# A gated convolution's input projection: c and u of tiles 2 to 5 by seven block products in place of plain products

## The chip, the cores and the metric

The kernel runs on one core of one Trainium2 chip. A time is the device time of one execution in microseconds (us). Of the kernel before there are three timed runs, 1012.52, 1012.60 and 1012.88 us, with a median of 1012.6. One more execution was recorded by the hardware profiler. Engines are called as the profile calls them: PE (TensorE), PEld (its weight loads), DVE (VectorE), ACT (ScalarE), POOL (GpSimd), SP (SyncE, which only issues loads here).

## The reference

The model has two layers of width 1024 on 512 tokens, in float32. The change lies in the first mixer, of which only the projection by `w_in` is computed in another way:

```python
def short_conv_mixer(h, w_in, conv_w, w_out):      # h = rmsnorm(x, a_pre_norm)
    bcx = h @ w_in                                 # 512x1024 @ 1024x3072
    b_gate, c_gate, u = jnp.split(bcx, 3, axis=-1)
    y = b_gate * causal_depthwise_conv3(c_gate * u, conv_w)
    return y @ w_out
# layer 0: h = h + rmsnorm(short_conv_mixer(...)); h = h + rmsnorm(swiglu(rmsnorm(h)))
# layer 1: k, v from rmsnorm(h) @ w_kv; sliding-window attention with sinks; swiglu
```

## The kernel before, in words

**Arithmetic.** A product of float32 matrices is made of three matmuls in the 32-bit round format: each operand is split into a rounded high part and the remainder, and `mm3` issues weight-high by x-low, weight-high by x-high, weight-low by x-high. The high part of a weight block (128x1024, 512 KB) is a copy on ACT (`whi<-raw`, L490 before), the low part a subtraction on DVE (`wlo<-raw,whi`, L491). A plain job is `project`: eight depth blocks by three, 24 matmuls of 128 weight columns against 512 tokens, into one PSUM bank of 128x512.

**The convolution's tiles.** The 1024 columns of c, u and b are cut in eight tiles f of 128 columns, which lie on partitions with the 512 tokens beside them. For each tile there are a c, a u and a b job. Behind them stand the steps of `conv`: `first` multiplies c's bank by the row factor `rows` (1 over the root mean square of each token's x, broadcast over the partitions by two matmuls into the bank `pr`), `second` does the same for u and forms cu = c times u, `taps` makes the three taps of the causal convolution on DVE (a scaling and two multiply-adds), `third` multiplies b's bank by `rows` and forms y. The two products cu and y run on GpSimd for the tiles 0 to 6 (`eng`). Tiles 0 and 1 are projected in the opening, while the first loads arrive, and their steps are left for the list `late`.

**The line.** The jobs of the tiles 2 to 7 stand in one line, in the order of the string `CONV`, with the products P1 to P7 of the first half of `w_out` (these were block products before already, made by `seven` with sums of y from `pair_sums`) and the splits w0 to w3 of the second half of `w_out` between. `in_line` walks it: after the products of job j it splits the weights of job j + 3 (`LINE_LEAD`), issues the loads whose buffer the job just split used last (seven raw buffers of 512 KB, `raw`), sums raw blocks for the job behind that one (`add`), takes a few steps from `late`, and then appends job j's own steps to `late`. There are four pairs of split weights. PSUM's banks come from three pools: `ps_mm` four, `ps_sc` two, `ps_pt` two.

**Order.** All engines run under a schedule written by hand: what the program writes first for an engine runs first on it. Weight loads are issued on SP's queue. GpSimd's queue also issues `hsum` transfers: copies and accumulations from DRAM to DRAM that make sums of blocks of the feed-forward weights `w_gb` and `w_dn` for later (class `Sums`, `sum_on`, `issue`, L559 before). In the convolution's line `sum_on(f"c{f}")` puts a group in the list, and `issue` writes it at once.

Of the kernel before, what the change touches and what calls it, by code (L numbers as in the profile page):

```python
# [16 lines left out]
P = 128  # L17
D = 1024
# [19 lines left out]
    "c2 u2 b2 c3 u3 b3 c4 u4 b4 c5 u5 P1 P5 b5 P6 P3 c6 P7 P2 u6 P4 b6 w0 c7 u7 w1 b7 w2 w3"  # L38
)

# [41 lines left out]
def yoco_kernel(  # L82
# [8 lines left out]
    w_in: bass.AP,  # L91
    w_ob: bass.AP,
# [134 lines left out]
    xt = [halves("xt") for _ in range(KT // 2)]  # L227
    xt = [xt[k // 2][k % 2] for k in range(KT)]
# [217 lines left out]
    class Raw:  # L446


        def __init__(self, *srcs):
            self.srcs = srcs  # L450
            self.widths = [s.shape[0] * S if len(s.shape) == 3 else D for s in srcs]
            self.n = sum(self.widths)

        def fetch(self):
            self.tile, c = wraw.tile([P, D], F32, tag="raw", name=name("raw")), 0
            for src, n in zip(self.srcs, self.widths):
                dst = self.tile[:, c : c + n]
                if len(src.shape) == 3:
                    src, dst = (src.rearrange("k p c -> p k c"),
                                dst.rearrange("p (k c) -> p k c", c=S))  # L460
                nc.sync.dma_start(dst, src)
                c += n

    class Job:
# [10 lines left out]
        def add(self):  # L475
            if self.make:
# [18 lines left out]
    def in_line(jobs, late, paced=True):  # L495
# [9 lines left out]
        def prepare(j):  # L505
# [3 lines left out]
            while n[0] < len(raws) and (n[0] < N_RAW or raws[n[0] - N_RAW].last <= j):  # L509
                raws[n[0]].fetch()  # L510
# [7 lines left out]
        for j, job in enumerate(jobs):  # L518
# [5 lines left out]
            for _ in range(1 if paced else max(len(late) - 1, 1)):  # L524
# [143 lines left out]
    rows = slot("rrow")  # L668
# [6 lines left out]
    sums = small.tile([P, 4], F32, tag="sums", name=name("sums"))  # L675
    squares = wide("squares")

    def square(b):
        nc.scalar.activation(squares, hs[b], AF.Square, scale=1 / 32,
                             accum_out=sums[:, b : b + 1])  # L680

    with tc.manual_schedule(engines=ALL):

        warm = small.tile([P, 1], F32, tag="warm", name=name("warm"))
        nc.scalar.activation(warm, ones[:, 0:1], AF.Copy)
        idle = bank("idle", ps_pt)
        for _ in range(WARM):
            nc.tensor.matmul(idle[:, :P], ones, ones, start=True, stop=True)

        def first_hi(i, c0, c1):  # L690
            nc.scalar.activation(ws[i][0][:, c0:c1], first[i][:, c0:c1], AF.Copy)

        def first_lo(i, c0, c1):
            nc.vector.tensor_tensor(out=ws[i][1][:, c0:c1], in0=first[i][:, c0:c1],
                                    in1=ws[i][0][:, c0:c1].bitcast(F32), op=ALU.subtract)

        def token_hi(k):
            nc.scalar.activation(xs[k][0], xt[k], AF.Copy, scale=g(G_APRE, k))

        def token_lo(k):  # L700
            nc.vector.scalar_tensor_tensor(
                out=xs[k][1], in0=xt[k], scalar=g(G_APRE, k), in1=xs[k][0].bitcast(F32),
                op0=ALU.mult, op1=ALU.subtract,
            )

        FIRST = {0: [(0, 0, P), (0, P, 384)], 1: [(0, 384, 768)], 2: [(0, 768, D), (1, 0, S)],
                 4: [(1, S, D)], 5: [(2, 0, S)], 6: [(2, S, D)]}
        for k in range(KT):
            pieces = FIRST.get(k, [])
            token_hi(k)  # L710
            for p in pieces:
                first_hi(*p)
            for p in pieces:
                first_lo(*p)
            token_lo(k)
            for i in range(3):
                for t in range(3):
                    n = 3 * k + t
                    whi, wlo = (w[:, n % KT * P : (n % KT + 1) * P] for w in ws[n // KT])
                    nc.tensor.matmul(begun[0][t], (whi, wlo, whi)[i], xs[k][i == 2],  # L720
                                     start=k == i == 0, stop=k == KT - 1 and i == 2)
        later += [fetch(w_in[1, t]) for t in range(len(later), 3)]
        for b in range(NB):
            hs[b] = wide("h")
            nc.sync.dma_start(hs[b], x[b])
        nc.sync.dma_start(mask, tables[:, 2 * S :])
        nc.sync.dma_start(snk, sinks.partition_broadcast(P))
        ws = [split_weights(None, raw, True) for raw in later[:2]]
        square(0)
        square(1)  # L730
        ws.append(split_weights(None, later[2], True))
        square(2)
        square(3)
        project(begun[1][0], ws[0], xs)
        v = small.tile([P, 4], F32, tag="v", name=name("v"))
        nc.vector.tensor_scalar(out=v, in0=sums, scalar1=EPS, scalar2=None, op0=ALU.add)
        nc.gpsimd.tensor_tensor(out=cols, in0=v, in1=mhalf, op=ALU.pow)
        project(begun[1][1], ws[1], xs)
        pr = bank("pr", ps_pt)
        dg, dhi, dlo = slot("dg"), slot("dhi", F32R), slot("dlo", F32R)  # L740
        for b in range(NB):
            nc.vector.tensor_scalar(out=dg[:, b * P : (b + 1) * P], in0=ident,
                                    scalar1=cols[:, b : b + 1], scalar2=None, op0=ALU.mult)
        nc.scalar.activation(dhi, dg, AF.Copy)
        nc.vector.tensor_tensor(out=dlo, in0=dg, in1=dhi.bitcast(F32), op=ALU.subtract)
        nc.tensor.matmul(pr, ones_r, dlo, start=True, stop=False)
        nc.tensor.matmul(pr, ones_r, dhi, start=False, stop=True)
        nc.scalar.activation(rows, pr, AF.Copy)
        nc.vector.tensor_scalar(out=nsnk, in0=snk, scalar1=-1.0, scalar2=None, op0=ALU.mult)
# [5 lines left out]
    def conv(f, pc=None, pu=None, pb=None):  # L755

        eng = nc.gpsimd if f < KT - 1 else nc.vector
        cr, ur = halves("cru")
        cu, t = halves("cut")
        br, y = halves("bry")  # L760
# [8 lines left out]
        def second(pu):  # L769
            nc.vector.tensor_tensor(out=ur, in0=pu, in1=rows, op=ALU.mult)  # L770
            eng.tensor_tensor(out=cu, in0=cr, in1=ur, op=ALU.mult)

        def taps():
            nc.vector.tensor_scalar(out=t, in0=cu, scalar1=g(G_CONV, 16 + f), scalar2=None,
                                    op0=ALU.mult)
# [6 lines left out]
        def third(pb):  # L782
            nc.vector.tensor_tensor(out=br, in0=pb, in1=rows, op=ALU.mult)
            eng.tensor_tensor(out=y, in0=t, in1=br, op=ALU.mult)
# [14 lines left out]

        return first, second, taps, third, end  # L800

# [34 lines left out]
    with tc.manual_schedule(engines=ALL):  # L836
        project(begun[1][2], ws[2], xs)

        def late():
            parts = []  # L840
            for f in range(2):
                first, second, taps, third, end = conv(f)
                first(begun[f][0])
                second(begun[f][1])
                parts += [taps, lambda third=third, f=f: third(begun[f][2])]
                sum_on(f"c{f}")
                issue(len(issues))
# [899 lines left out]
```

## Time and profile before

| what | value |
|---|---|
| runs, median (lowest to highest) | 1012.6 us (1012.52 to 1012.88) |
| the profiled execution | 1012.5 us; its span on the chip 1010.7 us |
| granted clock of TensorE, mean | 0.999 |
| instructions | 16083 |
| moved by DMA | 244.50 MB, 242 GB/s |
| GpSimd's transfers (software queue) | 96.48 MB, 37.6% of 16 engines' span |
| hardware queue of the loads | 145.98 MB, 38.8% |

The profile is of one execution. The span goes from the first to the last instruction recorded; what is not in it (1.8 us) lies around it. Busy times are sums of instruction times, and matmuls are pipelined, so one matmul's time is longer than the distance to the next; the distance between two starts, called pitch here, is what a matmul costs. A row of an engine in order of time gives the start, the length, the engine, the line, the operation, out<-in by the program's names, and the shape; in square brackets stands how long the engine was idle ahead of it and what ended that. A row of DMA issues gives the median time from issue to landing.

### The profile page before, as it was taken

To read this page: it belongs to the slowest core of one execution; us is meant where nothing else is said; L and a number is where in the kernel's file an instruction comes from. 1 tells how busy PE (TensorE), PEld (TensorE's weight loads), DVE (VectorE), ACT (ScalarE), POOL (GpSimd) and SP (SyncE) were. 2 spreads that over 40 slices of the span, in tenths; PEclk is the share of its full clock that TensorE was granted. 3 is DMA by queue.
4 is the path that set the end of the run, shared out by engine and by line. 5 is a ranking of instruction groups with operands and counts; after the bars stand their busy time and mean duration, and the time that the engine had idled before them with its cause. 6 is when DMAs were issued, how large, how long until landed. Compare 5 with 4: busy or idle time off the path is not lost.

```text
span 1010.7 us, 16083 instructions
## 1 busy us (share of the span) xinstructions
PE 1002.3 (99%) x5864; PEld 882.4 (87%) x5864; DVE 887.7 (88%) x1525; ACT 588.4 (58%) x1061; POOL 203.9 (20%) x264
## 2 busy tenths in 40 slices
PE   9999999999999999999999999999999999999997
PEld 8888888999889898898898888789998888989986
DVE  5766767899789999999888998888997999999996
ACT  6322444875656465566385788777666564645641
POOL 0443033102101011000022657321211010110001
PEclk9999999999999999999999999999999999999999
DMA  9997789649979789779603889966999577979742
GB/s 357 293 252 241 180 248 334 185 167 268 334 246 288 250 287 311 240 214 343 209 1 120 225 236 245 303 233 176 295 288 330 167 247 235 284 277 266 247 174 84
DMA packets 66575, 244.50 MB, mean 242 GB/s; under 512 B 7872, under 2 KB 8384, under 8 KB 54720
## 3 DMA queue, kind: packets, MB, share of 16 engines
q1 hardware_dynamic: 51328, 145.98, 38.8%
q0 software_dynamic: 14592, 96.48, 37.6%
q10 hardware_dynamic: 576, 1.02, 0.3%
q8 instruction: 46, 0.75, 0.3%
q14 instruction: 33, 0.27, 0.1%
HBM read 237.15 MB, written 102.76 MB: 336 GB/s over the span
## 4 chain that ended last, share of the span: by engine, by line
PE 97%; DVE 2%; ACT 1%; issue 0%; DVEq 0%
PE gx L1093 15%; PE gx L1096 8%; PE pcub L207 4%; PE pcub L205 4%; PE pcub L206 4%; PE px L206 4%; PE px L205 4%; PE px L207 4%; PE pmix L207 3%; PE pmix L205 3%; PE pmix L206 3%; PE gz L1093 3%; PE gy L206 2%; PE gy L205 2%; PE gy L207 2%; PE pz L206 2%
## 5 line engine op out<-in xcount | busy, mean ns | idle before, releaser
L491 DVE TENSOR_TENSOR wlo<-raw,whi 128x1024 fp32r<-128x1024 f32 x225 | 274.6, 1225 | 33.8 <-ACT whi L490 33.7
L490 ACT ACTIVATE whi<-raw 128x1024 fp32r<-128x1024 f32 x225 | 233.7, 1051 | 99.1 <-DVE raw L478 28.7
L1093 PE MATMUL gx<-xt,whi 128*128 128x512 f32 x480 | 120.7, 393 | 0.0
L1093 PEld LDWEIGHTS gx<-xt,whi 128*128 128x128 f32 x480 | 86.2, 189 | 15.7
L559 POOL DMA_DIRECT2D hsum<-in_w_gb_dram x96 | 64.4, 757 | 135.0 <-ACT whi L490 89.6
L559 POOL DMA_DIRECT2D hsum<-hsum x32 | 25.3, 792 | 304.8 <-ACT whi L490 219.7
L1048 DVE TENSOR_TENSOR st<-gx,st 128x256 f32<-128x256 f32 x200 | 77.5, 419 | 2.2 <-ACT st L1071 0.4
L1071 ACT ACTIVATE st<-gx 128x256 f32<-128x256 f32 x120 | 43.5, 380 | 60.9 <-PE gx L1096 57.2
L1096 PEld LDWEIGHTS gx<-xt,wlo 128*128 128x128 f32 x480 | 65.5, 190 | 4.7
L1096 PE MATMUL gx<-xt,wlo 128*128 128x256 f32 x480 | 66.9, 282 | 0.0
L1107 ACT ACTIVATE gr<-gr 128x1024 f32<-128x1024 f32 x20 | 21.2, 1062 | 55.6 <-DVE gr L1048 55.6
L205 PE MATMUL px<-wlo,ahi 128*128 128x512 f32 x120 | 46.7, 389 | 0.0
L206 PE MATMUL px<-whi,ahi 128*128 128x512 f32 x120 | 46.7, 389 | 0.0
L207 PE MATMUL px<-whi,alo 128*128 128x512 f32 x120 | 46.7, 389 | 0.0
L205 PE MATMUL gy<-xlo,whi 128*128 128x256 f32 x160 | 45.3, 283 | 0.0
L206 PE MATMUL gy<-xhi,whi 128*128 128x256 f32 x160 | 45.3, 283 | 0.0
L207 PE MATMUL gy<-xhi,wlo 128*128 128x256 f32 x160 | 45.3, 283 | 0.0
L559 POOL DMA_DIRECT2D hsum<-in_w_dn_dram x48 | 32.6, 794 | 47.3 <-ACT whi L490 47.3
L1093 PE MATMUL gx<-xhl,whi 128*128 128x512 f32 x160 | 39.9, 391 | 0.0
L312 POOL TENSOR_TENSOR ur<-uv,mhalf 128x1 f32<-128x1 f32 x15 | 13.9, 929 | 119.8 <-DVE uv L308 119.8
L660 DVE TENSOR_TENSOR mix<-mix,px 128x512 f32<-128x512 f32 x54 | 34.8, 682 | 2.2 <-PE px L207 2.2
L478 DVE TENSOR_TENSOR raw<-raw,raw 128x1024 f32<-128x1024 f32 x28 | 34.1, 1219 | 0.0
(322 smaller groups left out, 2996.8 us busy)
## 6 DMA issues: line engine op xcount, KB each, us to landing
hsum<-in_w_gb_dram POOLq DMA_DIRECT2D x96, 512.0 KB, 8.0
raw<-hsum SPq DMA_DIRECT2D x88, 512.0 KB, 7.9
raw<-in_w_gb_dram SPq DMA_DIRECT2D x60, 512.0 KB, 7.0
hsum<-in_w_dn_dram POOLq DMA_DIRECT2D x36, 512.0 KB, 8.2
raw<-in_w_dn_dram SPq DMA_DIRECT2D x32, 512.0 KB, 6.2
hsum<-hsum POOLq DMA_DIRECT2D x28, 512.0 KB, 5.7
raw<-in_w_in_dram SPq DMA_DIRECT2D x21, 512.0 KB, 7.4
hsum<-in_w_dn_dram POOLq DMA_DIRECT2D x12, 768.0 KB, 12.1
```

The lines of the kernel that those rows point to most:

```text
L205: nc.tensor.matmul(out, whi, xlo, start=start, stop=False, **kw)
L206: nc.tensor.matmul(out, whi, xhi, start=False, stop=False, **kw)
L207: nc.tensor.matmul(out, wlo, xhi, start=False, stop=stop, **kw)
L478: nc.vector.tensor_tensor(out=raw, in0=raw, in1=self.raws[1].tile, op=ALU.add)
L490: self.begun = nc.scalar.activation(hi[:, :n], raw, AF.Copy)
L491: nc.vector.tensor_tensor(out=lo[:, :n], in0=raw, in1=hi[:, :n].bitcast(F32), op=ALU.subtract)
L559: nc.gpsimd.dma_start(dst, src, max_dma_last_dim=4 * 4 * S, **kw))
L660: nc.vector.tensor_tensor(out=m, in0=m, in1=banks[bs][r], op=ALU.subtract if half else ALU.add)
L1048: nc.vector.tensor_tensor(out=out, in0=a, in1=b, op=ALU.add)
L1071: nc.scalar.activation(ste, a, AF.Copy)
L1093: nc.tensor.matmul(banks[c][e], whi[:, kk], factors[p][k][2], start=opened and k == 0, stop=False, **kw)
L1096: nc.tensor.matmul(banks[c][e][:, :256], wlo[:, kk], factors[p][k][0], start=False, stop=k == 3 and p in (4, 5), **kw)
```

## The change

For the tiles 2, 3 and the tiles 4, 5, c and u are no longer four plain products. The 1024x256 by 512 problem of each two tiles is cut in a 2x2 grid of blocks: depth halves of four, and c and u side by side in a block of the host-side array `w_cu`. Seven products of block sums take the place of eight. A job of such a product is 24 matmuls against 256 columns: two tiles e, four depth blocks k, three parts. X1 to X7 are the seven products of tiles 2, 3, and Y1 to Y7 those of tiles 4, 5. Their results accumulate in three banks (`gx`, `gz`, `gy`), and `take` combines these on ACT and DVE. All that this needs is added:

- In the opening x is scaled and combined in place in four sums of quarters (`scaled` on ACT, `combine` on DVE), which are split into high and low parts (`sum_hi` on ACT, `sum_lo` on DVE). These are 4, 16, 8 and 8 operations, all ahead of the line's first job. The squares of x are taken from half tiles (`own`), which they overwrite; x is loaded again from DRAM, four loads of 512 KB on SP's queue, behind Y4.
- Sums of weight blocks (`make_two`, `make_three`, `make_four`) on DVE, four of 128x1024 a pair.
- Neither c nor u is multiplied by `rows`; their product is multiplied by the squared factor `rows2` (`square_rows`). The first tap of the tiles 2 to 5 runs on ACT.
- The b jobs of these tiles (`gate_job`) are plain, and are multiplied by `rows` right behind their products.
- No cu or y product runs on GpSimd any more; all are DVE's. GpSimd keeps the small powers and its transfers.
- The positions at which the groups of `hsum` transfers enter the queue are new (b3's end, X3, Y6, Y3 for c2 to c5), and `late` is emptied by half its length a job instead of all but one.

```diff
-    "c2 u2 b2 c3 u3 b3 c4 u4 b4 c5 u5 P1 P5 b5 P6 P3 c6 P7 P2 u6 P4 b6 w0 c7 u7 w1 b7 w2 w3"
+    "b2 b3 X1 X2 X6 X5 X7 X3 X4 b4 Y1 Y2 Y6 b5 Y5 Y7 Y3 Y4 c6 P1 P5 P6 P3 u6 P7 P2 P4 b6 w0 c7 u7 w1 b7 w2 w3"
...
-            for _ in range(1 if paced else max(len(late) - 1, 1)):
+            for _ in range(1 if paced else max(len(late) // 2, 1)):
...
+    def scaled(k):
+        q = quarter(0, 1, k)
+        nc.scalar.activation(q, q, AF.Copy, scale=g(G_APRE, k))
+
+    def combine(k):
+        q11, q21, q12, q22 = (quarter(i, hf, k) for hf in range(2) for i in range(2))
+        g0, g1 = g(G_APRE, k), g(G_APRE, k + 4)
+        for out, a, sc, op, b in ((q11, q11, g0, ALU.subtract, q12),
+                                  (q12, q22, g1, ALU.subtract, q12),
+                                  (q22, q22, g1, ALU.add, q11),
+                                  (q21, q21, g1, ALU.subtract, q22)):
+            nc.vector.scalar_tensor_tensor(out=out, in0=a, scalar=sc, in1=b, op0=ALU.mult,
+                                           op1=op)
...
     def conv(f, gr=None, br=None):
-        eng = nc.gpsimd if f < KT - 1 else nc.vector
...
         def second(pu):
             nc.vector.tensor_tensor(out=ur, in0=pu, in1=rows, op=ALU.mult)
-            eng.tensor_tensor(out=cu, in0=cr, in1=ur, op=ALU.mult)
+            nc.vector.tensor_tensor(out=cu, in0=cr, in1=ur, op=ALU.mult)
+
+        def square_rows():
+            nc.vector.tensor_tensor(out=cu, in0=cu, in1=rows2, op=ALU.mult)
 
         def taps():
-            nc.vector.tensor_scalar(out=t, in0=cu, scalar1=g(G_CONV, 16 + f), scalar2=None,
-                                    op0=ALU.mult)
+            if gr is None:
+                nc.vector.tensor_scalar(out=t, in0=cu, scalar1=g(G_CONV, 16 + f),
+                                        scalar2=None, op0=ALU.mult)
+            else:
+                nc.scalar.activation(t, cu, AF.Copy, scale=g(G_CONV, 16 + f))
...
-            eng.tensor_tensor(out=y, in0=t, in1=br, op=ALU.mult)
+            nc.vector.tensor_tensor(out=y, in0=t, in1=br, op=ALU.mult)
...
+    BEGUN = {"X": {3: "c3"}, "Y": {6: "c4", 3: "c5"}}
+
+    def gate_job(f, pool):
+        def products(job):
+            ps = bank("pcub", pool)
+            project(ps, job.w, xs)
+            brs[f] = slot("bry")
+            nc.vector.tensor_tensor(out=brs[f], in0=ps, in1=rows, op=ALU.mult)
+        return Job([Raw(w_in[f, 2])], products, begin("c2") if f == 3 else None)
+
+    def cross_jobs(f, c):
+        a11, a12, a21, a22 = (Raw(w_cu[f // 2 - 1, b]) for b in range(4))
+        both_of = Raw()
+        pools = {"X": ps_mm, "Y": ps_pt, "Z": ps_sc}
+        chain = {1: "X", 6: "X", 7: "X", 4: "X", 5: "Z", 3: "Z", 2: "Y"}
...
+        def make_two():
+            plus(both_of, a21, a22)
+        def make_three():
+            plus(a21, a21, a11)
+            plus(a11, a11, both_of)
+        def make_four():
+            plus(a12, a12, a11)
+
+        raws = {1: [a11], 2: [a12, both_of, a21, a22], 6: [a11, a21, both_of], 5: [both_of],
+                7: [a21], 3: [a12, a11], 4: [a22]}
+        make = {2: make_two, 6: make_three, 3: make_four}
...
+        def take(p):
+            x, y, z = (banks.get(c) for c in "XYZ")
+            st, u, gr = kept
+            g0, g1 = (gr.rearrange("p (e h c) -> p e h c", e=2, h=2)[:, :, h] for h in range(2))
+            if p in (1, 6):
+                nc.scalar.activation(st, x, AF.Copy)
+            elif p == 5:
+                nc.scalar.activation(u, z, AF.Copy)
+            elif p == 2:
+                nc.vector.tensor_tensor(out=g0, in0=tiles(y), in1=tiles(st), op=ALU.add)
+            elif p == 3:
+                nc.vector.tensor_tensor(out=g1, in0=tiles(z), in1=tiles(st), op=ALU.add)
+            elif p == 7:
+                nc.vector.tensor_tensor(out=u, in0=x, in1=u, op=ALU.add)
+            else:
+                for gg, m in ((g0, x), (g1, u)):
+                    nc.vector.scalar_tensor_tensor(out=gg, in0=tiles(m), scalar=-1.0, in1=gg,
+                                                   op0=ALU.mult, op1=ALU.mult)
...
+        def end():
+            steps = [conv(f + e, kept[2], brs.pop(f + e)) for e in range(2)]
+            parts = [lambda: [s[0]() for s in steps], steps[0][1], steps[1][1],
+                     lambda: [s[2](None) for s in steps]]
...
+            if f + 2 == CROSS[1]:
+                for b in range(NB):
+                    hs[b] = wide("h")
+                    tc.keep_in_program_order(nc.sync.dma_start(hs[b], x[b]))
+            return parts
...
+    cu = wi[CROSS[0] : CROSS[1], :2].reshape(-1, 2, 2, P, 2, S).transpose(0, 2, 4, 3, 1, 5)
+        "w_cu": c(cu.reshape(-1, 4, P, D)),
```

Three places of the built order show what moves. In the rows, the line of the code, the operation, out<-in by the program's names with a buffer's number, and the shape. Lines of the changed kernel have other numbers: L559 is L566 there, L490 and L491 are L497 and L498.

GpSimd's queue from the row factor's power (`cols`) on; before:

```order
L737 TENSOR_TENSOR cols_233<-v_428,mhalf 128x4
L771 TENSOR_TENSOR cut_532<-cru_531 128x512
L559 DMA hsum_132<-in_w_gb_dram 64x2048
L559 DMA hsum_133<-in_w_gb_dram 64x2048
L559 DMA hsum_134<-in_w_gb_dram 64x2048
L559 DMA hsum_135<-in_w_gb_dram 64x2048
L771 TENSOR_TENSOR cut_543<-cru_542 128x512
L559 DMA hsum_132<-in_w_gb_dram 64x2048
```

The same place now:

```order
L801 TENSOR_TENSOR cols_234<-v_468,mhalf 128x4
L566 DMA hsum_132<-in_w_gb_dram 64x2048
L566 DMA hsum_133<-in_w_gb_dram 64x2048
L566 DMA hsum_134<-in_w_gb_dram 64x2048
L566 DMA hsum_135<-in_w_gb_dram 64x2048
L566 DMA hsum_132<-in_w_gb_dram 64x2048
L566 DMA hsum_133<-in_w_gb_dram 64x2048
L566 DMA hsum_136<-in_w_gb_dram 64x2048
```

The product that stood ahead of the first group (`cut<-cru`, which needs the row factor) is gone from the queue; 30 transfers stand behind each other before the queue's next instruction that an engine's result releases (`ur`, after the mixer).

ACT in the jobs of the tiles 4 and 5; before, the high parts of five jobs in a row:

```order
L490 ACTIVATE whi_677<-raw_509 128x1024
L490 ACTIVATE whi_717<-raw_511 128x1024
L490 ACTIVATE whi_751<-raw_517 128x1024
L490 ACTIVATE whi_784<-raw_523 128x1024
L490 ACTIVATE whi_827<-raw_529 128x1024
```

And now, from the high part of Y2 on (`t<-gr` are the first taps of the tiles 2 and 3, `st<-gx` the copies of the bank of Y1 and then of Y6):

```order
L497 ACTIVATE whi_924<-raw_795 128x1024
L497 ACTIVATE whi_963<-raw_589 128x1024
L851 ACTIVATE t_930<-gr_690,gt 128x512
L851 ACTIVATE t_932<-gr_690,gt 128x512
L933 ACTIVATE st_975<-gx_978 128x512
L497 ACTIVATE whi_1004<-raw_832 128x1024
L608 ACTIVATE a_235_935<-yy_931 128x256
L497 ACTIVATE whi_1040<-raw_797 128x1024
L618 ACTIVATE ahi_1046<-s_933 128x512
L933 ACTIVATE st_975<-gx_978 128x512
```

Between the splits stand now taps and copies, which wait for DVE and for PE.

DVE in the first jobs of the line; before:

```order
L491 TENSOR_TENSOR wlo_637<-raw_507,whi_636 128x1024
L612 TENSOR_TENSOR alo_643<-s_553,ahi_642 128x512
L612 TENSOR_TENSOR alo_647<-yy_534,ahi_646 128x512
L770 TENSOR_TENSOR cru_555<-pcub_611,rrow_232 128x512
L491 TENSOR_TENSOR wlo_678<-raw_509,whi_677 128x1024
L774 TENSOR_SCALAR cut_556<-cut_556,gt 128x512
L777 SCALAR_TENSOR_TENSOR cut_556<-cut_556,gt 128x511
L777 SCALAR_TENSOR_TENSOR cut_556<-cut_556,gt 128x510
L491 TENSOR_TENSOR wlo_718<-raw_511,whi_717 128x1024
```

And now, from b2's eviction (`bry<-pcub_607`) on; X2's split is the row after it, the `raw` rows are sums of weight blocks, and `bry<-pcub_243` with `yy` is tile 0's third step. X6's split stands two rows behind the last one shown:

```order
L896 TENSOR_TENSOR bry_632<-pcub_607,rrow_232 128x512
L498 TENSOR_TENSOR wlo_635<-raw_572,whi_634 128x1024
L909 TENSOR_TENSOR raw_575<-raw_575,raw_570 128x1024
L909 TENSOR_TENSOR raw_570<-raw_570,raw_574 128x1024
L848 TENSOR_SCALAR cut_554<-cut_554,gt 128x512
L853 SCALAR_TENSOR_TENSOR cut_554<-cut_554,gt 128x511
L853 SCALAR_TENSOR_TENSOR cut_554<-cut_554,gt 128x510
L860 TENSOR_TENSOR bry_555<-pcub_243,rrow_232 128x512
L861 TENSOR_TENSOR yy_556<-cut_554,bry_555 128x512
L848 TENSOR_SCALAR cut_558<-cut_558,gt 128x512
L853 SCALAR_TENSOR_TENSOR cut_558<-cut_558,gt 128x511
L853 SCALAR_TENSOR_TENSOR cut_558<-cut_558,gt 128x510
```

Two weight sums, tile 0's taps and third step and tile 1's taps stand between X2's split and X6's, where one tile's taps stood between two splits before.

313 lines of the change are left out of this document (206 added, 107 removed).

## The prediction

> **What bounds the kernel now.** I read the page first, then the chain that ended last, then TensorE (PE) and VectorE (DVE) in order of time through the stage that is edited.
>
> ```profile
> span 1010.7 us, 16083 instructions
> PE 1002.3 (99%) x5864; PEld 882.4 (87%) x5864; DVE 887.7 (88%) x1525; ACT 588.4 (58%) x1061; POOL 203.9 (20%) x264
> PE 97%; DVE 2%; ACT 1%; issue 0%; DVEq 0%
> ...
> sum 120.00, PE 120.00 PEld 99.33 DVE 83.89 ACT 38.64 POOL 39.14; mean PE 30.00 PEld 24.83 DVE 20.97 ACT 9.66 POOL 9.79
> ```
>
> The chain is TensorE for 97% of the span. The last line is the sum over 30 to 150 us, the convolution's line: TensorE has no gap there, VectorE has 36 us left of 120. So a matmul less is time gained, and each wait of TensorE is time lost; nothing later gives it back.
>
> **The matmuls.** First and last row of 24 wide products (one job), and of 48 products of 256 columns:
>
> ```profile
> 54.73 0.39 PE L205 MATMUL pcub<-xhl,whi 128*128 128x512 f32 x1
> ...
> 60.17 0.39 PE L205 MATMUL pcub<-xhl,whi 128*128 128x512 f32 x1
> ...
> 178.89 0.28 PE L205 MATMUL pgu<-xhl,whi 128*128 128x256 f32 x1
> ...
> 184.65 0.28 PE L205 MATMUL pgu<-xlo,whi 128*128 128x256 f32 x1
> ```
>
> (60.17 - 54.73) / 24 = 0.2267 us, (184.65 - 178.89) / 48 = 0.120 us. Removed are c and u of four tiles, 8 jobs of 24 wide matmuls, 192 x 0.2267 = 43.5 us. Added are 14 block products of 24 narrow ones, 336 x 0.120 = 40.3 us. Term one: **-3.2 us**, since a narrow matmul costs 53% of a wide one, not half. The Trainium skill (TensorE: Matmul & The Clock Gate, Back-to-back issue gap) speaks against the change: it gives a stream of weight loads and matmuls 81 ns at 128 columns and 131 ns at 512; my estimate from these is 98 ns at 256, and 336 x 98 against 192 x 131 would add 7.8 us. The trace disagrees, with 227 and 120 ns for just such streams, so the rows decide, and no chance is kept for it.
>
> **VectorE while X runs.** Rows for the pitch of its operations, and one beside a GpSimd product:
>
> ```profile
> 41.94 0.48 DVE L774 TENSOR_SCALAR cut<-cut,gt 128x512 f32<-128x512 f32 x1
> 42.45 1.54 DVE L777 SCALAR_TENSOR_TENSOR cut<-cut,gt 128x511 f32<-128x511 f32 x2
> 43.91 0.69 DVE L783 TENSOR_TENSOR bry<-pcub,rrow 128x512 f32<-128x512 f32 x1
> ...
> 47.48 0.41 DVE L605 TENSOR_TENSOR s<-yy 128x256 f32<-128x256 f32 x1
> ...
> 48.28 0.42 DVE L605 TENSOR_TENSOR s<-yy 128x256 f32<-128x256 f32 x1
> ...
> 50.27 1.22 DVE L491 TENSOR_TENSOR wlo<-raw,whi 128x1024 fp32r<-128x1024 f32 x1
> 51.40 0.68 DVE L612 TENSOR_TENSOR alo<-s,ahi 128x512 fp32r<-128x512 f32 x1
> 52.01 0.68 DVE L612 TENSOR_TENSOR alo<-yy,ahi 128x512 fp32r<-128x512 f32 x1
> ...
> 66.67 2.34 DVE L491 TENSOR_TENSOR wlo<-raw,whi 128x1024 fp32r<-128x1024 f32 x1 [0.17 <-ACT whi L490]
> ...
> 66.64 1.29 POOL L771 TENSOR_TENSOR cut<-cru 128x512 f32<-128x512 f32 x1 [5.79 <-DVE cru L770]
> ```
>
> Start to start: 1.13 us for 1024 elements (split or sum), 0.60 for 512, 0.40 for 256 (two in 0.80), 1.97 for three taps; one that reads the result before it waits out the 0.69. The last two rows show that a GpSimd product held a split for 1.1 us more; with the 14 products gone this is gained, but on VectorE, which had time to spare here.
>
> Per pair, the blocks cost VectorE 7 splits and 4 sums (11 x 1.13), five combinations (3.0) and two row products and two gatings (2.4): 17.8 us. They replace 4 splits, 4 evictions and 2 first taps (8.0). Two pairs: +19.6, and six products of tiles 0, 1, 6 add 3.6. In 120 us it fits; what counts is the 20.2 us of X (seven times 2.88), where the taps of tiles 0 and 1 stand in front. By hand, in the built order: b2 starts at 38.4 (32.47 below, two matmuls, 5.44), its last product is out at 44.0. From there to X5's split stand 1 eviction (0.60), X2's split (1.13), two sums, the second after the first (2.37), tile 0's taps, third and gating (3.28), tile 1's taps (1.97), an eviction (0.60), X6's split (1.13), tile 1's third and gating (1.31) and three operations of 256 (1.15): 13.5 us. So X5's split runs from 57.5 to 58.7. TensorE reaches X5 at 57.9 and needs the low part at its third matmul, 58.15: it waits 0.6. The same way X7's split ends at 61.9 against 61.65 (0.2), X3's at 65.35 against 64.8 (0.6). Term two: **+1.4 us**, from 0.4 (pitches 0.1 us shorter on ten operations) to 2.5.
>
> **The opening.**
>
> ```profile
> 14.49 2.44 ACT L189 ACTIVATE whi<-raw 128x512 fp32r<-128x512 f32 x4
> ...
> 19.30 0.18 ACT L679 ACTIVATION_READ_ACCUMULATOR squares<-h 128x1 f32 x1
> ...
> 49.88 0.61 ACT L611 ACTIVATE ahi<-s 128x512 fp32r<-128x512 f32 x1
> 50.40 0.62 ACT L611 ACTIVATE ahi<-yy 128x512 fp32r<-128x512 f32 x1
> 50.92 1.05 ACT L490 ACTIVATE whi<-raw 128x1024 fp32r<-128x1024 f32 x1
> ...
> 26.97 0.16 DVE L736 TENSOR_SCALAR v<-sums 128x4 f32<-128x4 f32 x1
> ...
> 31.35 0.68 DVE L745 TENSOR_TENSOR dlo<-dg,dhi 128x512 fp32r<-128x512 f32 x1
> ...
> 33.76 0.69 DVE L767 TENSOR_TENSOR cru<-pcub,rrow 128x512 f32<-128x512 f32 x1 [1.64 <-ACT rrow L748]
> ...
> 32.47 0.39 PE L746 MATMUL pr<-dlo,ones_r 128*128 128x512 f32 x1
> ```
>
> ScalarE (ACT) is free of `whi` at 16.9. Then come 4 scalings of 256 (at most 0.52 each), 8 half squares (0.52 + 0.18), 2 splits and 4 high parts before the last square: 27.8, so `v` at 27.9, 0.9 later than 26.97. The two wide splits that stood ahead of `dlo` are gone, four low parts of 512 stand there, and `dlo` is done at 32.0, in time for 32.47: nothing, covered by 0.4 us. Then four more low parts (2.4) and six operations on tiles 0 and 1 (3.8) precede b2's split, which ends at 38.6 if they start as the row at 33.76 does, at 39.5 if they start at 34.6; TensorE wants it at 38.85. Ends 0 and 0.7: I take **+0.3**, nearer the row.
>
> **The loads of Y, where the change is decided.** The sums of gate blocks are DMAs on GpSimd's queue. Before, each group stood behind a product and so behind a row factor; now only the queue's own earlier DMAs hold them:
>
> ```profile
> 36.36 2.23 POOL L559 DMA_DIRECT2D hsum<-in_w_gb_dram  x4
> ...
> 56.19 1.77 POOL L559 DMA_DIRECT2D hsum<-in_w_gb_dram  x2
> ...
> 68.40 1.28 POOL L559 DMA_DIRECT2D hsum<-in_w_gb_dram  x2
> ...
> 58.83 0.34 SPq L461 DMA_DIRECT2D raw<-in_w_in_dram  x1
> 62.54 0.37 SPq L461 DMA_DIRECT2D raw<-in_w_ob_dram  x1
> 69.04 0.34 SPq L461 DMA_DIRECT2D raw<-in_w_in_dram  x1
> 73.37 0.37 SPq L461 DMA_DIRECT2D raw<-in_w_ob_dram  x1
> ...
> raw<-in_w_in_dram SPq DMA_DIRECT2D x1, 512.0 KB, 10.9
> ...
> raw<-in_w_ob_dram SPq DMA_DIRECT2D x1, 512.0 KB, 8.5
> ...
> raw<-in_w_in_dram SPq DMA_DIRECT2D x1, 512.0 KB, 8.7
> ...
> raw<-in_w_ob_dram SPq DMA_DIRECT2D x1, 512.0 KB, 6.9
> ...
> raw<-in_w_out_dram SPq DMA_DIRECT2D x1, 512.0 KB, 3.5
> ...
> raw<-hsum SPq DMA_DIRECT2D x1, 512.0 KB, 15.1
> ```
>
> The loads at 58.83, 62.54, 69.04 and 73.37 landed after 10.9, 8.5, 8.7 and 6.9 us, with GpSimd's transfers in flight; one at 119.8, with none, after 3.5; one at 149, behind nine of them, after 15.1. The four took 80.3 - 58.8 = 21.5 us, 5.4 each. In the new program the queue starts at 28 (behind `cols`) and has 30 transfers to issue before it meets a wait on an engine, so it is full through X and Y.
>
> Y's blocks a12, a21, a22 wait for buffers that X5's split, X7's split and X3's sum release: issued at 58.7, 61.9 and 63.0. If they were alone, a22 would land at about 67; by the 15.1 row at 78. By 5.4 each from 58.7 the third comes at 75.0 at the earliest, since it is issued 4.3 us after the first: I take 76.
>
> TensorE ends X4 at 71.1 (69.4 + 0.3 + 1.4), b4 at 76.6, Y1 at 79.5, and wants Y6 at 82.3. Y6 adds into the bank of Y1, whose copy stands on ScalarE behind tiles 2 and 3's first taps, and these behind VectorE: from a22's landing the a21 + a22 sum (1.13), X4's two closings (1.2), Y2's split (1.13), two sums (2.3), ScalarE's high part of Y6 (1.1, b4's eviction beside it), its low part (1.13), a row product (0.69), two taps on ScalarE (1.04) and the copy (0.62): 10.4 us. 76 + 10.4 = 86.4: term four, **+4.1 us**, from 0 (landing by 71.9) to 6.2 (at 78.1). Without that order on ScalarE the path would be Y6's high part, 6.9 us after the landing, and the wait 0.6.
>
> Free of charge: the second reading of x (2 MB on SP, four loads behind `w0`'s): first use is the residual update after 160 us, some 50 us later. First taps of tiles 2 to 5 on ScalarE: 4 x 0.52 on an engine with 81 of 120 us free, but for the place above. The jobs behind Y (P, c6 to w3) are unchanged and find the transfers further on than before: 0, up to 1.5 if their loads are starved too.
>
> **Sum.** -3.2 + 0.3 + 1.4 + 4.1 = +2.6 us. The profiled execution took 1012.5 (span 1010.7 and 1.8 around it), 0.1 below the median of 1012.6: **1015.2 us**. A measurement of this kernel tells about 0.2% (2.0 us) from no change.
>
> **Rivals.**
> 1. The loads are in time (a22 by 71.9). For it: alone they take 3.5 us; GpSimd's chain waits on its own transfers and leaves holes. Against: the four rows above. It gives -3.2 + 0.3 + 1.4 = -1.5, 1011.1: not slower. It decides from a landing 9 us after issue.
> 2. VectorE keeps up as well, since no GpSimd product holds it: the full -3.2, 1009.4. Against: the 13.5 us list has no such product in it and is late all the same.
> 3. The starving goes on: b5, c6 and the P blocks wait too, as the 15.1 row allows: +6.2 and more beside the rest, 1018 to 1021.
>
> **How the numbers follow.** Forecast (a22 between 74 and 78, 1013.2 to 1017.3): 0.55, of it 0.13 within 0.2% (landing before 75.4). Rival 1: 0.20, of it 0.03 faster. Rival 2: 0.08, faster. Rival 3: 0.17, slower. Faster 0.11, within 0.2% 0.30, slower 0.59. The range leaves out rival 2 and the far half of rival 3: 1010.7 to 1018.9.
>
> **What would show it.** Right: TensorE rows `gx` or `gz` of X and Y at 0.120 us pitch; small gaps before X5, X7 and X3 released by VectorE's `wlo`; one gap of 2 to 6 us in Y before Y6, released by ScalarE's copy of `gx`; hsum transfers from about 28 us on; loads of w_cu around 60 us that take over 9 us. Wrong: no gap in Y (rival 1), a gap before the second `pr` product (the opening), or gaps in P (rival 3).

## The result and the profile after

The changed kernel took 1018.49 us (median of 4 runs, 1017.52 to 1018.98), the kernel before 1012.61: a ratio of 1.0056 with a 95% interval of 1.0043 to 1.0068. It is slower, by 5.9 us where 2.6 were forecast.

The page of the profile after, its span, its busy times and the chain that ended last:

```profile
span 1016.6 us, 16446 instructions
PE 1002.4 (99%) x6008; PEld 887.5 (87%) x6008; DVE 918.1 (90%) x1575; ACT 606.6 (60%) x1098; POOL 184.2 (18%) x250
PE 88%; DVE 6%; DMA 3%; ACT 2%; issue 1%; DVEq 0%; SPq 0%; ACTq 0%
...
sum 120.00, PE 114.57 PEld 100.40 DVE 103.54 ACT 52.08 POOL 18.45; mean PE 114.57 PEld 100.40 DVE 103.54 ACT 52.08 POOL 18.45
```

The chain was TensorE for 97% before, with VectorE at 2%; now it is 88%, with VectorE at 6% and a DMA at 3%. The last line is the window from 30 to 150 us: TensorE is idle for 5.4 us of it, VectorE went from 83.9 to 103.5 us (the forecast's sum is 83.9 + 19.6 + 3.6 = 107.1 for the whole line, which now reaches past the window). What TensorE waited for, up to 180 us (engine, line, what it waited for: us in total, times, longest):

```profile
PE gx L208 <- ACT st L933: 3.8, 1, 3.8
PE idle L742 <- DVE ones L152: 1.1, 1, 1.1
PE gz L210 <- DVE wlo L498: 0.7, 2, 0.5
PE pz L208 <- DVE wlo L498: 0.5, 1, 0.5
PE pcub L774 <- ACT whi L745: 0.4, 1, 0.4
PE px L208 <- DVE mix L667: 0.4, 1, 0.4
```

`idle` and `pcub L774` lie in the first 6 us; the kernel before has the first of them as well (1.1 us), not the second. The others, in TensorE's rows in order of time:

```profile
39.15 0.50 PE L210 MATMUL pcub<-xhl,wlo 128*128 128x512 f32 x1
...
59.34 0.38 PE L210 MATMUL gz<-xf,wlo 128*128 128x256 f32 x1 [0.47 <-DVE wlo L498]
...
65.84 0.38 PE L210 MATMUL gz<-xhi,wlo 128*128 128x256 f32 x1 [0.28 <-DVE wlo L498]
...
86.61 0.58 PE L208 MATMUL gx<-xf,whi 128*128 128x256 f32 x1 [3.79 <-ACT st L933]
86.99 0.41 PE L209 MATMUL gx<-xf,whi 128*128 128x256 f32 x1
87.20 0.41 PE L210 MATMUL gx<-xf,wlo 128*128 128x256 f32 x1
...
90.82 0.40 PE L208 MATMUL pcub<-xhl,whi 128*128 128x512 f32 x1
...
122.12 0.47 PE L208 MATMUL pz<-wlo,ahi 128*128 128x512 f32 x1 [0.54 <-DVE wlo L498]
...
136.34 0.50 PE L208 MATMUL px<-wlo,ahi 128*128 128x512 f32 x1 [0.37 <-DVE mix L667]
...
183.08 0.48 PE L208 MATMUL pmix<-wlo,yhi 128*128 128x512 f32 x1
```

The same `pmix` product starts at 177.44 in the kernel before, so 5.6 us of the difference lie ahead of it. Counted from start to start, above the pitches of 0.2267 and 0.120 us:

| place | forecast | measured |
|---|---|---|
| fewer and narrower matmuls | -3.2 | -3.2 |
| b2's low part (39.15) | +0.3 | +0.26 |
| X: X5, X7, X3 | +1.4 | +1.55 (0.47 and 0.28 of it idle by the rows, X7 0.1) |
| Y6, the gap | +4.1 | +3.95 |
| Y6, its matmuls behind the gap: 90.82 - 86.61 = 4.21 for 24 of 0.120 | none | +1.33 |
| the products P (122.12 and 136.34) | 0, up to 1.5 | +1.40 |
| a later start of the opening's last stage, and small gaps | none | +0.3 |

What made Y6 wait, in the rows of SP, VectorE, ScalarE and GpSimd:

```profile
59.32 0.33 SPq L464 DMA_DIRECT2D raw<-in_w_cu_dram  x1
62.32 0.33 SPq L464 DMA_DIRECT2D raw<-in_w_cu_dram  x1
63.46 0.33 SPq L464 DMA_DIRECT2D raw<-in_w_cu_dram  x1
raw<-in_w_cu_dram SPq DMA_DIRECT2D x1, 512.0 KB, 12.1
60.66 2.34 POOL L566 DMA_DIRECT2D hsum<-in_w_dn_dram  x4
...
75.72 1.23 DVE L909 TENSOR_TENSOR raw<-raw,raw 128x1024 f32<-128x1024 f32 x1 [5.04 <-DMA raw<-in_w_cu_dram]
...
84.74 1.33 ACT L851 ACTIVATE t<-gr,gt 128x512 f32<-128x512 f32 x2 [1.89 <-DVE gr L844]
85.98 0.57 ACT L933 ACTIVATE st<-gx 128x512 f32<-128x512 f32 x1
```

The three loads are a12, a21 and a22 of Y. They landed after 4.2, 8.7 and 12.1 us (the DMA row is that of the last): the four copies of `w_dn`, 768 KB each, left between the first and the second. VectorE waited 5.0 us and began the a21 + a22 sum at 75.7; ScalarE waited for the row products, took the two first taps, and only then copied Y1's bank: 85.98, and Y6 began at 86.6.

P's waits begin with a late load too. Ahead of a sum of P, VectorE waited 1.6 us for a block of `w_out`, and the taps of tiles 4 and 5 and P3's split stand behind that sum:

```profile
112.21 1.23 DVE L485 TENSOR_TENSOR raw<-raw,raw 128x1024 f32<-128x1024 f32 x1 [1.57 <-DMA raw<-in_w_ob_dram]
```

### The profile page after: what moved, and what is told of

It reads as the page before. It is cut to its first block, busy times and chain, and to the rows that moved or that the text cites. A ratio compares the mean times of both kernels' runs of the same rounds, so it can differ in the third digit from the quotient of the medians.

```text
span 1016.6 us, 16446 instructions
## 1 busy us (share of the span) xinstructions
PE 1002.4 (99%) x6008; PEld 887.5 (87%) x6008; DVE 918.1 (90%) x1575; ACT 606.6 (60%) x1098; POOL 184.2 (18%) x250
## 4 chain that ended last, share of the span: by engine, by line
PE 88%; DVE 6%; DMA 3%; ACT 2%; issue 1%; DVEq 0%; SPq 0%; ACTq 0%
PE gx L1285 15%; PE gx L1288 8%; PE px L208 3%; PE px L209 3%; PE px L210 3%; PE pmix L210 3%; PE pmix L209 3%; PE pmix L208 3%; PE gz L1285 3%; PE gy L209 2%; PE gy L208 2%; PE gy L210 2%; PE pcub L774 2%; PE pz L210 2%; PE pz L209 2%; PE pz L208 2%
## 5 line engine op out<-in xcount | busy, mean ns | idle before, releaser
L497 ACT ACTIVATE whi<-raw 128x1024 fp32r<-128x1024 f32 (+1 forms) x231 | 239.7, 1051 | 109.9 <-DVE raw L485 40.5
L498 DVE TENSOR_TENSOR wlo<-raw,whi 128x1024 fp32r<-128x1024 f32 (+1 forms) x231 | 279.8, 1215 | 22.4 <-ACT whi L497 22.3
L566 POOL DMA_DIRECT2D hsum<-in_w_gb_dram x96 | 63.3, 719 | 149.3 <-ACT whi L497 89.1
L566 POOL DMA_DIRECT2D hsum<-hsum x32 | 25.2, 788 | 329.3 <-ACT whi L497 222.2
L1299 ACT ACTIVATE gr<-gr 128x1024 f32<-128x1024 f32 x20 | 21.2, 1061 | 55.8 <-DVE gr L1240 55.8
L208 PE MATMUL gy<-xlo,whi 128*128 128x256 f32 x176 | 49.8, 283 | 0.0
L209 PE MATMUL gy<-xhi,whi 128*128 128x256 f32 x176 | 49.8, 283 | 0.0
L210 PE MATMUL gy<-xhi,wlo 128*128 128x256 f32 x176 | 49.8, 283 | 0.0
L566 POOL DMA_DIRECT2D hsum<-in_w_dn_dram x48 | 31.9, 745 | 57.2 <-ACT whi L497 45.7
```

Source lines behind the costliest of these rows:

```text
L208: nc.tensor.matmul(out, whi, xlo, start=start, stop=False, **kw)
L209: nc.tensor.matmul(out, whi, xhi, start=False, stop=False, **kw)
L210: nc.tensor.matmul(out, wlo, xhi, start=False, stop=stop, **kw)
L497: self.begun = nc.scalar.activation(hi[:, :n], raw, AF.Copy)
L498: nc.vector.tensor_tensor(out=lo[:, :n], in0=raw, in1=hi[:, :n].bitcast(F32), op=ALU.subtract)
L566: nc.gpsimd.dma_start(dst, src, max_dma_last_dim=4 * 4 * S, **kw))
```

## The experiments

All edits are to the changed kernel but for one, which is to the kernel before. The theory: Y6 waits because a22 lands late, GpSimd's transfers make it late, and the order on ScalarE lengthens the way from there; X waits for VectorE alone. The rivals: the transfers alone, the order alone, or GpSimd's lost products as such.

**All groups of transfers held (e1_pace).**

```diff
-            issue(len(issues))
+            issue(len(issues), latest[0])     # behind the high part written last
```

> The changed kernel with each group of GpSimd's transfers of the tiles 0 to 5 held until ScalarE has begun the high part that was written last before it. So the 768 KB copies that it issued at 60.7 us, and that made a22 land 12 us after its issue, come behind Y6's products. Theory (the wait of Y6 comes from a22's landing, and that from these transfers): a22 lands within 5 us, the 3.8 us wait and the slow matmuls behind it (1.45 us) go, 1018.5 - 5.2 = 1013.3 if nothing is given back. The same theory with a rider: the held transfers now lie beside the second reading of x and the last weights of the line, so a load of 15 us appears between 110 and 160 us and TensorE waits there for 3 to 10 us: 1016 to 1023. Rival (the order on ScalarE alone makes the wait): the copy of Y1's bank still stands behind the taps, the wait of Y6 stays above 3 us, 1018.

1023.94 us, 1.0109 (1.0095 to 1.0123). Y's wait is gone, and so are those of P; a longer one came at c7:

```profile
148.23 0.80 PE L208 MATMUL pcub<-xhl,whi 128*128 128x512 f32 x1 [9.56 <-ACT whi L499]
...
118.13 1.47 SPq L464 DMA_DIRECT2D raw<-in_w_in_dram  x2
...
h<-in_x_dram SPq DMA_DIRECT2D x4, 512.0 KB, 35.3
raw<-in_w_in_dram SPq DMA_DIRECT2D x3, 512.0 KB, 28.9
```

The rider was right in the place and the length of the wait (3 to 10 us were named); the time is 0.9 us above its range. From 100 us on the four readings of x took 35.3 us each and the loads of `w_in` behind them on SP's queue 28.9. The transfers made Y6's wait, since it goes when they are held; but they have to be moved at some time, and at this later place they cost more.

**First taps on VectorE (e2_taps).**

```diff
-                nc.scalar.activation(t, cu, AF.Copy, scale=g(G_CONV, 16 + f))
+            nc.vector.tensor_scalar(out=t, in0=cu, scalar1=g(G_CONV, 16 + f), ...)
```

> The changed kernel with the first taps of the tiles 2 to 5 on VectorE, as before; so Y1's copy stands directly behind Y2's high part on ScalarE. If the order on ScalarE were the whole cause, Y6's wait and its slow matmuls go and four taps of 0.48 us come to VectorE: 1018.5 - 3.3 - 1.45 = 1013.8. If the loads are the cause and the order only sets where they are felt: Y6 waits 0.6 us for its high part (a22 landed at 75.6, 6.9 us of work behind it), and b5, whose load landed at 84.9, waits next for its low part, 1 to 3 us: 1015 to 1018, with a new row of VectorE's wlo ahead of the bank pcub near 88 us.

1020.23 us, 1.0076 (1.0063 to 1.0089), above every bound that was named. The new row at b5 was there:

```profile
84.30 0.39 PE L208 MATMUL gx<-xf,whi 128*128 128x256 f32 x1 [1.16 <-ACT st L930]
...
91.36 0.67 PE L210 MATMUL pcub<-xhl,wlo 128*128 128x512 f32 x1 [2.91 <-DVE wlo L498]
```

Y6 waited 1.2 us for the copy, and b5 2.9 us for a low part that stood behind the row products and the taps of tiles 2 and 3. Both low parts, Y6's and b5's, stand in one list of VectorE, and between them it is longer by two first taps of 0.48 us. The edit moved the wait, and the slow matmuls with it.

**Products of tiles 0, 1 and 6 on GpSimd (e3_gps), and all products of the kernel before on VectorE (e4_bdve).**

```diff
+        eng = nc.gpsimd if gr is None and f < KT - 1 else nc.vector      # e3, and eng for cu and y
-        eng = nc.gpsimd if f < KT - 1 else nc.vector                     # e4
+        eng = nc.vector
```

> The changed kernel with the products of tiles 0, 1 and 6 on GpSimd again (six products of 0.6 us leave VectorE, and GpSimd's queue waits for the first ones). Theory (VectorE makes X's waits): the waits before X5 and X3 (0.47 and 0.28 us) go, and the queue starts later by the 36.4 - 28.9 us that the rows of before show: 1016 to 1017. Rival: the product on GpSimd takes 1.3 us where VectorE takes 0.6, and holds a split of VectorE for 1.1 us beside it (66.67 in the trace of before), and what needs y waits: X's waits grow to 1 us each, 1019 to 1021.

> The kernel before with its fourteen products on VectorE, nothing else changed: the part of the change that frees GpSimd's queue, alone. Theory: the loads are starved here too (the queue starts at 28 us and never waits for an engine in this line), but a plain job asks for 512 KB in 5.4 us and not in 2.9, and there is no sum ahead of a split, so TensorE waits little: 1012.6 to 1014, loads of w_in near 60 us that take over 10 us. If the free queue alone costs the time: 1016 or more.

The first took 1020.20 us, 1.0074 (1.006 to 1.0088), in the rival's range. X5 waited 1.00 us in place of 0.47, since VectorE waited 1.2 us for tile 1's y from GpSimd, while X3's wait stayed at 0.28 us. Y2 waited 0.8 us and Y6 4.4, and the waits of P were gone. What it shows of the loads is in two rows of VectorE and GpSimd:

```profile
78.24 1.23 DVE L910 TENSOR_TENSOR raw<-raw,raw 128x1024 f32<-128x1024 f32 x1 [6.70 <-DMA raw<-in_w_cu_dram]
78.28 2.35 POOL L566 DMA_DIRECT2D hsum<-in_w_dn_dram  x4
```

The copies of `w_dn` left only when the a21 + a22 sum had begun, and yet VectorE had waited 6.7 us for the blocks. So it need not be these copies: here the loads met the sums of `w_gb` alone, of which six transfers left between 58 and 65 us.

The second took 1012.67 us, 1.0000 (0.9991 to 1.0009). Two of its loads near 60 us:

```profile
raw<-in_w_ob_dram SPq DMA_DIRECT2D x1, 512.0 KB, 12.6
raw<-in_w_in_dram SPq DMA_DIRECT2D x1, 512.0 KB, 10.8
```

They were late as expected, and no matmul waited for them: a plain line asks for 512 KB in 5.4 us, three jobs ahead, and sums no blocks first. So the loads of the changed kernel take no longer than those that the kernel before bears on a freed queue; what is new is that a product needs three of them at once.

**The one group that ends with the copies of `w_dn` held, behind Y2's high part (e5_hold).** The edit is shortened here; `latest` lists the instructions of the high parts.

```diff
-            issue(len(issues))
+            issue(len(issues), latest[-5] if at == "c4" else None)
```

> The changed kernel with one group of GpSimd's transfers, the one that ends with the four 768 KB copies of w_dn, held behind the high part of Y2; all other groups as they are. In the changed kernel these copies left at 60.7 us, between the issues of Y's a12 (59.3) and a21 (62.3). Theory (a22's landing makes Y6's wait, and these copies make the landing; held for some 10 us they do no harm later, as they did when held until 85 us and later): a22 lands within 5 us, Y6 waits under 0.5 us, its slow matmuls (1.45 us) go with it, and the waits of the products P go or stay: 1018.5 - 5.4 - (0 to 1.4) = 1011.7 to 1013.1. If the held copies come back at the end of the line as in the run that held all groups: over 1016.

1014.46 us, 1.0015 (1.0007 to 1.0024). The issue of the last load and what all three took, the copies, and TensorE's first wait behind X:

```profile
63.68 0.33 SPq L464 DMA_DIRECT2D raw<-in_w_cu_dram  x1
raw<-in_w_cu_dram SPq DMA_DIRECT2D x1, 512.0 KB, 4.3
71.29 2.65 POOL L569 DMA_DIRECT2D hsum<-in_w_dn_dram  x4
...
115.07 0.50 PE L208 MATMUL px<-wlo,ahi 128*128 128x512 f32 x1 [1.24 <-ACT mix L668]
```

With the copies 10.6 us later the loads took 3.6, 3.3 and 4.3 us, and Y6 did not wait. So in the changed kernel this group, four copies and two sums of `w_gb` ahead of them, makes the late landing. The time is 1.4 us above the expected range, and P accounts for it: its waits grew to 1.24, 0.73 and 0.37 us, start to start 3.1 us in place of 1.4 (in a profiled execution 0.9 us above the median), since VectorE now waited 3.3 us for a block load of `w_out`.

**One step of `late` a job (e6_one), with the copies held too (e7_both).**

```diff
-            for _ in range(1 if paced else max(len(late) // 2, 1)):
+            for _ in range(1):
```

> The changed kernel with one step of the list `late` a job in place of half the list, so that the steps of tiles 0 and 1 spread over X and Y, and the taps of tiles 2 and 3 stand behind Y1's copy on ScalarE. Theory (X's waits are VectorE's, from the steps of tiles 0 and 1 in a row; Y6's wait is a late load whose effect the order on ScalarE enlarges): X's 1.55 us go, X5's and X7's splits release their buffers a microsecond earlier, so a21 and a22 are issued ahead of the copies of w_dn, Y6 waits under 1 us: 1018.5 - 1.55 - 5.2 = 1011.7, less up to 1.4 for P. Rival (the transfers alone): X's waits go, Y6's wait stays at 3 us or more: 1016 to 1017. Against the run with the taps on VectorE: there Y6's wait turned into one at b5, so an order that moves the wait and no load would show it again at b5 (pcub, wlo): 1016.

> Both edits at once: one step of `late` a job and the copies of w_dn held behind Y2's high part. Theory: no wait of TensorE is left in X and Y, and the 3.2 us of fewer matmuls show, but for what the products P and the opening still wait: 1009.5 to 1011, faster than before. If the two edits remove the same wait, the sum is that of the better one alone.

1010.59 us, 0.9978 (0.997 to 0.9987), and 1011.04 us, 0.9983 (0.9974 to 0.9992). The first is faster than the kernel before, and than the changed one by 7.9 us; the two don't differ by more than their intervals. In e6_one TensorE waits for nothing between the start and 180 us:

```profile
PE idle L742 <- DVE ones L152: 1.1, 1, 1.1
PE pcub L774 <- ACT whi L745: 0.4, 1, 0.4
PE pt L1604 <- DVE plo L1621: 0.4, 1, 0.4
...
55.77 0.33 SPq L464 DMA_DIRECT2D raw<-in_w_cu_dram  x1
59.47 1.47 SPq L464 DMA_DIRECT2D raw<-in_w_cu_dram  x2
62.16 2.34 POOL L566 DMA_DIRECT2D hsum<-in_w_dn_dram  x4
...
71.16 1.22 DVE L909 TENSOR_TENSOR raw<-raw,raw 128x1024 f32<-128x1024 f32 x1
175.40 0.48 PE L208 MATMUL pmix<-wlo,yhi 128*128 128x512 f32 x1
```

(The three waits are of the whole program; `pt` lies far behind.) Tile 0's and 1's steps no longer stand in a row between X2's and X5's splits, so X5 doesn't wait; its split and X7's release their buffers earlier, a12 to a22 leave at 55.8 to 60.6 us, all ahead of the copies of `w_dn`, and the sum begins at 71.2 in place of 75.7. (The last of them, issued 1.5 us ahead of the copies, still took 10.0 us.)

**TensorE kept at work in the gap (e8_warm).**

```diff
+                if c == "Y" and p == 2 and f == 4:
+                    idle = bank("idle", ps_sc)
+                    for _ in range(32):
+                        nc.tensor.matmul(idle[:, :256], whi[:, :P], factors[2][0][0], start=True, stop=True)
```

> The changed kernel with 32 products of 256 columns into a spare bank between Y2 and Y6, whose result nobody reads: TensorE has work in the 4.0 us in which it waited. Theory (the 16 matmuls at 0.21 us behind the wait are TensorE's clock, which goes down while it is idle): they run at 0.120 us again, 1018.5 - 1.45 = 1017.0, granted clock 0.999. Rival (Y6's own operands or the transfers beside it slow them): the pitch stays at 0.21 us and the time at 1018.5.

1017.25 us, 1.0046 (1.0034 to 1.0059). Windows of 86.6 to 89.5 us, the changed kernel and this one (after the engines' busy times, the column before the DMA share is the granted clock):

```profile
86.60:89.50 2.90, 2.89 (x13) 2.89 (x14) 2.87 (x4) 0.90 (x1) 1.22 (x3) 0.51 1.02 184
...
86.60:89.50 2.90, 2.90 (x25) 2.90 (x26) 2.86 (x5) 0.73 (x1) 0.97 (x2) 1.00 1.03 184
```

Thirteen matmuls at half the clock, and 25 at the full one beside the same DMA traffic. Y6 itself began as late as before (86.44). So TensorE's idle time is what halves its clock, and the cost is read from the rows: 1.33 us. The medians differ by 1.24 us, but the two intervals overlap.

**The one-step rule in halves: up to X7 (e9_x), from X3 on (e10_y).**

```diff
+            for _ in range(1 if paced else 1 if j < 7 else max(len(late) // 2, 1)):   # e9
+            for _ in range(1 if paced else 1 if j > 6 else max(len(late) // 2, 1)):   # e10
```

> The changed kernel with one step of `late` a job in the first seven jobs of the line alone (up to X7), then half the list as it was; so the steps of tiles 0 and 1 are spread, and the taps of tiles 2 and 3 stand ahead of Y1's copy again. It tells which half of the one-step rule removed Y6's wait. If the earlier issue of Y's loads did (a22's sum began at 71.2 there, 75.7 in the changed kernel): X's 1.55 us go, Y6 waits under 1 us, 1011 to 1012. If the order on ScalarE did: X's 1.55 us go, the copy still waits for VectorE's taps, Y6 waits 2.5 to 3.5 us and its clock goes down as well: 1015.5 to 1017.

> The other half: half the list in the first seven jobs as in the changed kernel, one step a job from X3 on. X's waits (1.55 us) stay and Y's loads are as late as in the changed kernel; but Y1's copy stands ahead of the taps on ScalarE, and the taps of tiles 2 and 3 behind Y6's low part on VectorE. If the order is the cause: Y6 waits 1 to 1.3 us (its high and low part, 6.9 us behind a22's landing), its clock stays, and b5 doesn't wait, since the taps that stood ahead of its split in the run with all taps on VectorE come later: 1018.5 - 4.2 - (0 to 1.4 for P) = 1012.9 to 1014.3. If the loads are: Y6 or b5 waits 3 us as there: 1016 and more.

1011.96 us, 0.9996 (0.9987 to 1.0005), and 1014.00 us, 1.0012 (1.0003 to 1.0021). TensorE's row at Y6 in e9_x, then VectorE's sum and TensorE's row in e10_y:

```profile
82.01 0.39 PE L208 MATMUL gx<-xf,whi 128*128 128x256 f32 x1 [0.40 <-ACT st L933]
...
76.57 1.23 DVE L909 TENSOR_TENSOR raw<-raw,raw 128x1024 f32<-128x1024 f32 x1 [5.87 <-DMA raw<-in_w_cu_dram]
...
84.24 0.39 PE L208 MATMUL gx<-xf,whi 128*128 128x256 f32 x1 [1.16 <-ACT st L933]
```

Either half removes most of Y6's wait. In e9_x the taps still stand ahead of the copy, but the loads are early; in e10_y the loads are as late as in the changed kernel (sum at 76.6), but the copy stands ahead of the taps. So the wait needed the late landing and the order together, and each had its own price: 0.4 us for the order with early loads, 1.2 and 0.3 us for the landing with a good order. P's waits are gone in e10_y. There the taps of tiles 4 and 5 come two at a time and not four (2.98 us) ahead of P3's split, but VectorE doesn't wait for a block of `w_out` either, so this run doesn't say which of the two did it. In e9_x the four taps stand in a row as in the changed kernel, VectorE waits 0.44 us for the block in place of 1.57, and no wait of P is left.

**Two other parts undone with the one-step rule: first taps on VectorE (e11_taps), products of tiles 0, 1, 6 on GpSimd (e12_gps).** The edits are those of e2_taps and e3_gps.

> The changed kernel with one step of `late` a job throughout, and the first taps of tiles 2 to 5 on VectorE: one part of the change undone where nothing waits in X and Y. If VectorE is short there: four taps of 0.48 us put splits late, TensorE waits 0.5 to 1.5 us in Y and P: 1011 to 1012.2 against the 1010.6 of the run with one step a job. If VectorE has room: 1010.6.

> The changed kernel with one step of `late` a job throughout, and the products of tiles 0, 1 and 6 on GpSimd again: another part undone. In the run that undid it in the changed kernel itself the time rose by 1.7 us, X5's wait from 0.47 to 1.00. If that was the place of the products (all in a row there), spread steps hide it: 1010.6. If GpSimd's 1.3 us a product and the 1.1 us by which it holds a split are paid wherever they stand: 1011 to 1012.

1011.62 us, 0.9989 (0.998 to 0.9998), and 1011.13 us, 0.9985 (0.9976 to 0.9993). Each has one wait more than e6_one, 0.83 us before a product of P (`mix`) and 0.63 us before X4 (`st`, the step behind X7). As medians both are slower than e6_one, by 1.0 and 0.5 us; the intervals overlap with its own, so only the waits are shown, not a time.

## Why the prediction was right, and where it was short

The measured 1018.5 us lie near the upper end of the stated range, but 1.2 us above the forecast's own branch (1013.2 to 1017.3) and in that of rival 3. The four terms of the sum were right in place and, all in all, in size; what lifts the time to 1018.5 was not in the sum.

*The matmuls.* Right: the pitches of `gx` and `gz` are 0.120 us (59.68 to 59.80 in the rows of X), and the -3.2 us fit the run in which nothing waits. In e6_one the `pmix` row stands at 175.40, 2.0 us ahead of before, though its last opening stage began 0.4 us later (22.00 against 21.59): -2.04 = -3.2 + 0.4 + 0.76. The 0.76 us are what is left over; the rows show 0.56 of them as three small gaps (at 39.6, 67.3 and 128.7 us).

*VectorE in X, and the opening.* Right in place, engine and size. X5's low part held the third matmul, as forecast; counted from start to start X5 lost 0.7 us where the list gave 0.6, X3 0.5 where it gave 0.6, X7 0.1 where it gave 0.2. What the prediction missed is that this lateness also moved Y's loads. It took the issue times of a12 to a22 from X's late splits, but priced X and Y as separate terms; e6_one and e9_x show what lay in between: TensorE felt 0.5 us of X5's late split, but the buffers came free 2.9 to 3.6 us later than they could (59.3 against 55.8 for a12), which put two of the loads behind the copies of `w_dn` and so made most of Y's wait.

*The loads of Y.* Right: the sum was forecast to begin at 76, and began at 75.7; Y6 was to start at 86.4, and started at 86.6. The releaser was ScalarE's copy. The mechanism was tested from three sides: without the copies in the way (e5_hold), with earlier issues (e9_x) and with another order (e10_y) the wait shrinks to 0, 0.4 and 1.4 us. The sentence that without the order on ScalarE the wait would be 0.6 gave less than half of what was measured (1.2 + 0.3), and left out that b5 is next in line (e2_taps). The loads were taken to land 5.4 us apart, at 64.1, 69.5 and 74.9 us; they landed at 63.5, 71.0 and 75.6.

*The missing 3.3 us.* The step that failed is that a wait was priced by its length alone. TensorE's clock fell to half behind the gap, which cost 1.33 us more. In the trace before the longest wait of TensorE is 1.1 us, so the price could not be read there; that there is one could, since the clock falls to 0.50 at 1008.6 us, 4.7 us behind the last matmul, where no work follows.

The Trainium skill states the rule (TensorE: Matmul & The Clock Gate, Part 1: The HAM clock gate): after a window of about 3.4 us without work the clock is halved, and comes back after about as long at work. The runs agree in kind, with a spread around that figure: the clock fell 3.0 to 4.8 us behind the last matmul and was back 2.8 to 5.5 us after the next (the waits of 2.9, 3.8, 4.4 and 9.6 us); waits of 0.4 to 1.2 us left it at 1.00. The wait of 2.9 us (e2_taps) was just long enough: there the clock fell at 91.5 us, as b5 started.

The second part is the term "0, up to 1.5 if their loads are starved too" of the P products, taken at 0, which was 1.40. Its own condition came true: VectorE waited 1.57 us for a block of `w_out`. Where it waited 3.3 us (e5_hold) P lost 3.1 us, and where it waited for none (e1_pace, e3_gps, e6_one, e10_y) P lost at most 0.2. Four taps in a row didn't make P wait by themselves, since e1_pace and e3_gps have them too; what their order adds to a late load was not tested alone, and longer taps on VectorE can make P wait without one (e11_taps). So rival 3 was right on P, and its 1018 to 1021 holds the time, but not by its mechanism alone: b5 did not wait, and the clock is nearly a quarter of the whole loss.

*Rivals 1 and 2.* Both are refuted as forecasts: the loads were late, and VectorE did not keep up. But both come true together with one number of the change altered (e6_one), and that kernel ends near rival 2's 1009.4.

*Not settled.* The second reading of x was only seen to hurt where transfers were pushed to it (e1_pace); moving it alone was not tried. The 0.26 us at b2 were not tested either, and the 0.4 us in the start of the opening's stage vary from run to run.

## What to carry to other kernels

When products are merged into blocks, the bytes stay the same but the deadlines don't: a product that needs three loads at once feels the last one, and every buffer it holds delays the next set. Price a wait of TensorE with the clock behind it, and follow a late split to the buffer that it releases, since that sets when the next load leaves and what it meets in the queues. If a list of side work is drained in bursts, spread it before judging the change: here one number turned 5.9 us lost into 2.1 us gained.

## What was not expected of the hardware

- TensorE's clock at half rate after one gap: 0.51 granted for 2.9 us behind 3.8 us of idle time, and 0.50 for 5.4 us behind 9.6 us (e1_pace) and for 5.5 us behind 4.4 us (e3_gps); a row of wide matmuls then costs 0.43 us each in place of 0.2267.
- Loads of 512 KB took 3.3 to 4.3 us with none of GpSimd's transfers in flight (e5_hold), and 8.6 to 13.0 us with four of 768 KB that had left 1.1 to 2.9 us ahead of them (the changed kernel, e2_taps, e8_warm, e10_y). They took 9.8 to 13.8 us with transfers of 512 KB alone (e3_gps), and 28.9 us behind four loads of the same queue with GpSimd's transfers in flight (e1_pace).
